# One PSUM bank of the mixer goes from the projections to the transposes of the attention weights

## The chip, the cores and the metric

The kernel runs on one core of a Trainium2 chip. The time is the device time of one launch, in microseconds (us), as the median of three runs. TensorE is PE in the profile, VectorE is DVE, ScalarE is ACT and GpSimd is POOL; PEld is the loading of PE's weights, which runs beside its matmuls. PE's results land in PSUM, which has eight banks; a bank holds 128 x 512 numbers of 32 bits, and ACT or DVE reads it out to SBUF.

## The reference

One layer of a hybrid block on 2048 tokens of width 1024, in float32:

```
h = rms_norm(x);  u = h @ w_in                    # 1024 -> 2560 columns: x, g, q, k, v
y_lru = gelu(u_g) * rg_lru(conv4(u_x))            # two 512 x 512 block-diagonal gates, a scan over tokens
z = q k^T / 8                                     # 8 heads of 64
att = exp(log_sigmoid(z) + suffix_sum(log_sigmoid(-z)))   # strictly causal, stick-breaking
y_att = att @ v
x = x + concat(rms_norm(y_lru), rms_norm(y_att)) @ w_out
x = x + swiglu(rms_norm(x)) @ w_ffn_out           # inner width 2816
out = rms_norm(x)
```

## The kernel before, in words

The first half of the kernel, up to about 1240 us, is the mixer: everything up to `w_out`. The rest is the FFN, which uses other PSUM pools.

Every matrix product is made of three matmuls with float32r operands, the high part times the high part and the two cross terms (`mm3`, lines 149 to 151). So each operand has to be split into a high part, which ACT copies, and a low part, which DVE or POOL subtracts.

The mixer works on four groups of 512 tokens. For each group, `prep` makes the projections. Its ten column groups stand in `GROUPS`: x, v, k, g, x, q, v, g, k, q. `make_ht` (line 207) turns the normalised tokens by PE transposes. `proj_col` (tile `pj`) makes one 128-column tile with 24 matmuls; `proj_v` (tile `pv`) makes one tile of values with 24 shorter ones; `Lru.gates` (tile `pg`) makes a gate tile with 3. Every one of these tiles, those of the transposes (`htp`, `h2t`), of the output projection (`po`) and of its sums (`pss`) is a bank of the pool `ps_d`. Such a bank is read out by ACT, DVE or both: a column of q or k by ACT line 290 and then DVE line 291; a tile of values by lines 315 and 316; a gate by ACT line 517; a turned tile by lines 208 and 209; an output tile by DVE line 671. The columns of x go by ACT line 495 into the convolution (ACT 498, DVE 500 three times, ACT 504).

The attention works on items: 128 queries by up to 512 keys. Each passes four stages, on different engines: `score` (matmuls into `z`, two sigmoids on ACT, a mask on POOL on the diagonal), `scan` (DVE line 372), `weights` (DVE line 378) and `turn`. `turn` (line 393) turns the weights by up to four PE transposes into a bank of the pool `ps_t` (tile `t`), which ACT copies (line 394, `ah`) and from which DVE subtracts (line 395, `al`). `weigh` then multiplies with the values into the one bank of `ps_y`. `LAGS` sets how far the stages run ahead: the scores four items before the turn.

`drive` interleaves the attention of group g with the projections of group g+1 (with the output projection for the last group), a few matmuls at a time. PE's order is exactly the order in which this is written. DVE, ACT, POOL and the DMA queue get their order from a scheduler, which takes the ready instruction of highest priority; attention steps get a priority ahead of their place. All engines then work strictly in that order. A pool does not hand out its banks in turn: a new tile gets a bank that is free, and its first matmul waits until the last reader of that bank's tile before is done.

Of the kernel before, what the change touches and what calls it, by code (L numbers as in the profile page):

```python
# [14 lines left out]
PSUM = bass.MemoryType.PSUM  # L15
# [75 lines left out]
def tile_block(ctx: ExitStack, tc: tile.TileContext, x, w_in, w_out, w_gu, w_dn,  # L91
# [62 lines left out]
    base = ExitStack()  # L154
# [1 line left out]
    htp = base.enter_context(tc.tile_pool(name="htp", bufs=KD, side="left"))  # L156
    wp = base.enter_context(tc.tile_pool(name="wp", bufs=WB, side="left"))
    stg = base.enter_context(tc.tile_pool(name="stg", bufs=4, side="left"))
    ps_d = base.enter_context(tc.tile_pool(name="ps_d", bufs=3, space=PSUM, side="left"))
    mix = ExitStack()  # L160
    lrp = mix.enter_context(tc.tile_pool(name="lrp", bufs=1, side="right"))
    atp = mix.enter_context(tc.tile_pool(name="atp", bufs=2, side="right"))
    kvp = mix.enter_context(tc.tile_pool(name="kvp", bufs=6, side="right"))
    ps_z = mix.enter_context(tc.tile_pool(name="ps_z", bufs=2, space=PSUM, side="right"))
    ps_t = mix.enter_context(tc.tile_pool(name="ps_t", bufs=2, space=PSUM, side="right"))
    ps_y = mix.enter_context(tc.tile_pool(name="ps_y", bufs=1, space=PSUM, side="right"))

    wg_hi = lrp.tile([P, NCT, 2, P], F32R, name="wg_hi")
# [1104 lines left out]
```

## Time and profile before

| | |
|---|---|
| runs | 2610.23, 2612.49, 2614.08 us; median 2612.49 us |
| profiled execution | 2616.12 us, span 2614.4 us |
| PE, PEld | 92%, 78% of the span busy |
| DVE, ACT, POOL | 70%, 48%, 45% |
| mean granted clock of PE | 0.97 of full |
| mixer | from 0 to about 1240 us |

The profiled execution is one launch. A row of the timeline says when an instruction (or a run of equal ones) started, how long it took, and in brackets how long its engine had been idle and what ended the wait. A row of the waits adds such idle times: total, how many, the longest. A busy share is an average over the span: what a change in one stage is worth has to be read in that stage.

### The profile page before, as it was taken

To read this page: it belongs to the slowest core of one execution; us is meant where nothing else is said; L and a number is where in the kernel's file an instruction comes from. 1 tells how busy PE (TensorE), PEld (TensorE's weight loads), DVE (VectorE), ACT (ScalarE), POOL (GpSimd) and SP (SyncE) were. 2 spreads that over 40 slices of the span, in tenths; PEclk is the share of its full clock that TensorE was granted. 3 is DMA by queue.
4 is the path that set the end of the run, shared out by engine and by line. 5 is a ranking of instruction groups with operands and counts; after the bars stand their busy time and mean duration, and the time that the engine had idled before them with its cause. 6 is when DMAs were issued, how large, how long until landed. Compare 5 with 4: busy or idle time off the path is not lost.

```text
span 2614.4 us, 36856 instructions
## 1 busy us (share of the span) xinstructions
PE 2417.2 (92%) x12680; PEld 2046.0 (78%) x12680; DVE 1837.1 (70%) x2569; ACT 1258.0 (48%) x2277; POOL 1174.2 (45%) x1397
## 2 busy tenths in 40 slices
PE   7999999998888887998799979979999999999998
PEld 5888788787778787888577758868888887788886
DVE  4566888999999999898645546686566562544557
ACT  5656677676766665665433323343333332332334
POOL 5855433223244221112565565464555454644443
PEclk9999999999999999999899989989999999999999
DMA  7787887664556565654333453252332326755563
GB/s 254 254 289 254 268 264 228 197 210 164 163 182 204 176 200 174 218 177 138 128 133 129 150 196 110 90 199 89 109 113 93 102 92 263 272 174 173 195 200 145
DMA packets 221804, 468.57 MB, mean 179 GB/s; under 512 B 22704, under 2 KB 63664, under 8 KB 221616
## 3 DMA queue, kind: packets, MB, share of 16 engines
q1 hardware_dynamic: 221616, 466.21, 53.1%
q8 instruction: 100, 1.64, 0.3%
q14 instruction: 88, 0.72, 0.1%
HBM read 333.74 MB, written 132.38 MB: 178 GB/s over the span
## 4 chain that ended last, share of the span: by engine, by line
PE 43%; DVE 3%; DMA 2%; POOL 2%; issue 2%; ACT 1%; SPq 0%; POOLq 0%; DVEq 0%; ACTq 0%
PE pw L151 5%; PE pw L150 5%; PE pw L149 5%; PE psc L149 3%; PE psa L149 3%; PE psc L150 3%; PE psc L151 3%; PE psa L150 3%; PE psa L151 3%; PE psd L149 3%; PE psd L150 3%; PE psd L151 3%; PE psb L149 1%; PE psb L150 1%; PE psb L151 1%
## 5 line engine op out<-in xcount | busy, mean ns | idle before, releaser
L360 POOL MEMSET u<- 128x1 f32 x320 | 31.2, 99 | 558.0 <-DVE u L372 393.4
L372 DVE TENSOR_TENSOR_SCAN u<-u,u,zero 128x513 f32<-128x513 f32 x192 | 255.5, 1332 | 9.0 <-ACT u L362 8.5
L393 PE MATMUL t<-ident,be 128*128 128x128 f32 x1088 | 180.2, 282 | 55.2 <-DVE al L395 46.2
L378 DVE TENSOR_TENSOR be<-be,u 128x512 f32<-128x512 f32 (+2 forms) x320 | 215.2, 675 | 17.0 <-POOL be L366 1.4
L362 ACT ACTIVATE u<-z 128x512 f32<-128x512 f32 (+2 forms) x320 | 172.4, 539 | 96.8 <-PE z L358 61.2
L149 PE MATMUL pj<-ht_hi,w_hi 128*128 128x512 f32 x512 | 214.9, 420 | 2.3 <-DVE sl L291 1.5
L394 ACT CAST ah<-t 128x512 fp32r<-128x512 f32 (+2 forms) x320 | 168.7, 527 | 87.0 <-PE t L393 81.6
L393 PEld LDWEIGHTS t<-ident,be 128*128 128x128 f32 x1088 | 131.7, 144 | 94.1 <-DVE al L395 60.5
L151 PE MATMUL pj<-ht_hi,w_lo 128*128 128x512 f32 x512 | 202.3, 395 | 0.0
L150 PE MATMUL pj<-ht_lo,w_hi 128*128 128x512 f32 x512 | 202.0, 395 | 0.0
L358 PE MATMUL z<-ks,qd 128*128 128x512 f32 (+2 forms) x640 | 191.1, 380 | 6.8 <-ACT be L363 5.2
L395 DVE TENSOR_TENSOR al<-t,ah 128x512 fp32r<-128x512 f32 (+2 forms) x320 | 191.1, 598 | 7.1 <-ACT ah L394 6.7
L1089 POOL TENSOR_TENSOR e<-c,c 128x512 f32<-128x512 f32 x110 | 158.7, 1451 | 50.5 <-DVE c L1080 36.8
L363 ACT ACTIVATE be<-z 128x512 f32<-128x512 f32 (+2 forms) x320 | 172.6, 539 | 0.2
L408 PE MATMUL y<-ah,vs 128*128 128x256 f32 x576 | 149.6, 290 | 13.9 <-DVE yp L418 13.9
L149 PE MATMUL po<-wo_hi,yhi 128*128 128x256 f32 x512 | 156.3, 305 | 0.0
L372 DVE TENSOR_TENSOR_SCAN u<-u,zero 128x129 f32<-128x129 f32 (+3 forms) x128 | 112.1, 877 | 57.0 <-POOL u L366 55.4
L1142 DVE TENSOR_TENSOR blo<-dr,bhi 128x1024 fp32r<-128x1024 f32 (+1 forms) x41 | 83.1, 2029 | 94.5 <-ACT bhi L1141 94.5
L1142 POOL TENSOR_TENSOR a0lo<-act,a0hi 128x1024 fp32r<-128x1024 f32 (+1 forms) x41 | 99.4, 2424 | 110.6 <-ACT a0hi L1141 110.6
L408 PE MATMUL y<-al,vs 128*128 128x256 f32 x576 | 147.2, 286 | 0.0
L150 PE MATMUL po<-wo_lo,yhi 128*128 128x256 f32 x512 | 146.6, 286 | 0.0
L151 PE MATMUL po<-wo_hi,ylo 128*128 128x256 f32 x512 | 146.6, 286 | 0.0
(283 smaller groups left out, 7564.3 us busy)
## 6 DMA issues: line engine op xcount, KB each, us to landing
r<-in_w_gu SPq DMA_DIRECT2D x88, 512.0 KB, 4.1
act<-act_d SPq DMA_DIRECT2D x68, 512.0 KB, 4.1
dr<-in_w_dn SPq DMA_DIRECT2D x59, 512.0 KB, 4.5
act_d<-e SPq DMA_DIRECT2D x110, 256.0 KB, 2.0
w_hi<-w_d SPq DMA_DIRECT2D x50, 512.0 KB, 4.7
w_lo<-w_d SPq DMA_DIRECT2D x50, 512.0 KB, 5.6
vs<-vs_d SPq DMA_DIRECT2D x80, 256.0 KB, 3.6
ks<-ks_d SPq DMA_DIRECT2D x80, 256.0 KB, 3.6
```

The costliest lines, as they stand in the source:

```text
L149: nc.tensor.matmul(ps, lhsT=w_hi, rhs=m_hi, start=first, stop=False, skip_group_check=more)
L150: nc.tensor.matmul(ps, lhsT=w_hi, rhs=m_lo, start=False, stop=False, skip_group_check=more)
L151: nc.tensor.matmul(ps, lhsT=w_lo, rhs=m_hi, start=False, stop=last, skip_group_check=more)
L358: nc.tensor.matmul(z[:, :nz], lhsT=qd[:, i, qs], rhs=kss[p.c][:, :nz], start=i == 0, stop=i == 1)
L362: nc.scalar.activation(u[:, :n], z[:, :n], AF.Sigmoid, scale=-SCALE)
L363: nc.scalar.activation(be[:, :n], z[:, :n], AF.Sigmoid, scale=SCALE)
L372: nc.vector.tensor_tensor_scan(out=ur, data0=ur, data1=zero.broadcast_to([P, n + 1]), initial=1.0 if p.prev is None else p.prev.u[s][:, 0: ...
L378: nc.vector.tensor_tensor(out=p.be[s][:, :n], in0=p.be[s][:, :n], in1=p.u[s][:, 1:n + 1], op=ALU.mult)
L393: nc.tensor.transpose(tp[:, b, :], p.be[s][:, b * P:(b + 1) * P], ident)
L395: nc.vector.tensor_tensor(out=alo[:, :nb, s, :], in0=tp[:, :nb, :], in1=f32(ahi[:, :nb, s, :]), op=ALU.subtract)
L408: nc.tensor.matmul(y, lhsT=vs[:, b, :], rhs=t[:, b].rearrange("p s q -> p (s q)"), start=first and m == 0, stop=last and m == 1)
L1142: eng.tensor_tensor(out=lo, in0=src, in1=f32(hi), op=ALU.subtract)
```

## The change

Of the eight banks of the mixer, `ps_d` had three, `ps_z` two, `ps_t` two and `ps_y` one. Now `ps_d` has two and `ps_t` three. Nothing is added or removed.

```
-    ps_d = base.enter_context(tc.tile_pool(name="ps_d", bufs=3, space=PSUM, side="left"))
+    ps_d = base.enter_context(tc.tile_pool(name="ps_d", bufs=2, space=PSUM, side="left"))
...
-    ps_t = mix.enter_context(tc.tile_pool(name="ps_t", bufs=2, space=PSUM, side="right"))
+    ps_t = mix.enter_context(tc.tile_pool(name="ps_t", bufs=3, space=PSUM, side="right"))
```

PE's instructions stand in the same order in both programs. The orders of DVE, ACT, POOL and the DMA queue differ in places. Two of ACT's and one of DVE's matter below.

On ACT at the start of the program, where the turned tokens of group 0 (`htp0_2` to `htp0_7`) are read out and the weights of the first projection are split:

```order
 L208 ACTIVATE ht_hi0_3_464<-htp0_3_466,gm_377 128x512
+L226 CAST w0_8_0_hi_534<-w0_8_0_raw_536 128x1024
 L208 ACTIVATE ht_hi0_4_473<-htp0_4_475,gm_377 128x512
-L226 CAST w0_8_0_hi_534<-w0_8_0_raw_536 128x1024
 L208 ACTIVATE ht_hi0_5_482<-htp0_5_484,gm_377 128x512
+L226 CAST w0_8_1_hi_543<-w0_8_1_raw_545 128x1024
 L208 ACTIVATE ht_hi0_6_491<-htp0_6_493,gm_377 128x512
 L208 ACTIVATE ht_hi0_7_500<-htp0_7_502,gm_377 128x512
-L226 CAST w0_8_1_hi_543<-w0_8_1_raw_545 128x1024
```

Two splits of weights have moved ahead of read-outs: the first by one read-out, the second by two.

On ACT at the end of the first group's projections, where the last column (`pj0_5_1`) and the last two turned tiles of group 1 are read out and the attention starts:

```order
 L290 CAST sh0_11_1705<-pj0_5_1_1626 128x512
 L208 ACTIVATE ht_hi1_6_1713<-htp1_6_1715,gm_377 128x512
+L208 ACTIVATE ht_hi1_7_1722<-htp1_7_1724,gm_377 128x512
 L362 ACTIVATE u0_0_0_0_0_1744<-z0_0_0_0_0_1741 128x128
 L363 ACTIVATE be0_0_0_0_0_1740<-z0_0_0_0_0_1741 128x128
-L208 ACTIVATE ht_hi1_7_1722<-htp1_7_1724,gm_377 128x512
```

The last tile's read-out has moved ahead of the first two sigmoids of the attention.

On DVE during the projections of group 1, where a column of k (`pj1_4_0`) is read out between the steps of the attention of group 0; the program before:

```order
L494 COPY xpad2_0_3975<-halo_252 128x3
L372 SCALAR_TENSOR_TENSOR u0_4_1_0_1_2785<-u0_4_1_0_1_2785,zero_67 128x513
L378 TENSOR_TENSOR be0_4_1_0_1_2781<-be0_4_1_0_1_2781,u0_4_1_0_1_2785 128x512
L418 TENSOR_TENSOR yp0_1_2544<-y0_3_0_0_2796,yb0_3_0_0_2801 64x256
L395 TENSOR_TENSOR al0_4_0_0_2820<-t0_4_0_0_0_2823,ah0_4_0_0_2819 128x128
L291 TENSOR_TENSOR sl1_8_2831<-pj1_4_0_2759,sh1_8_2830 128x512
L372 SCALAR_TENSOR_TENSOR u0_5_0_0_0_2856<-u0_5_0_0_0_2856,zero_67 128x129
```

The changed program has the same rows here, in the same order: the read-out `sl1_8` has not moved.

## Rows read from the trace of the kernel before

**Rows 1.** The page: busy time (share of the span) and instructions.
```profile
PE 2417.2 (92%) x12680; PEld 2046.0 (78%) x12680; DVE 1837.1 (70%) x2569; ACT 1258.0 (48%) x2277; POOL 1174.2 (45%) x1397
```

**Rows 2.** Windows: stretch, length, busy PE, PEld, DVE, ACT, POOL, PEclk, DMA share, GB/s.
```profile
27.00:150.00 123.00, 119.18 (x622) 100.97 (x621) 60.22 (x79) 68.84 (x103) 90.29 (x94) 1.00 0.79 263
150.00:300.00 150.00, 144.71 (x814) 123.58 (x814) 105.82 (x186) 96.71 (x202) 87.48 (x180) 1.00 0.79 266
300.00:520.00 220.00, 210.52 (x1263) 181.12 (x1261) 195.21 (x306) 151.01 (x313) 68.78 (x187) 0.99 0.74 238
520.00:800.00 280.00, 252.31 (x1499) 213.91 (x1497) 265.04 (x381) 195.79 (x385) 87.90 (x229) 0.98 0.56 182
800.00:1250.00 450.00, 385.97 (x2849) 361.20 (x2847) 412.54 (x677) 272.21 (x555) 105.18 (x261) 0.93 0.56 186
...
900.00:950.00 50.00, 38.60 (x267) 34.94 (x267) 43.41 (x84) 33.08 (x68) 6.70 (x28) 0.83 0.66 217
```

**Rows 3.** Waits of PE from 27 to 520 us: total us, times, longest.
```profile
PE t L393 <- DVE al L395: 5.6, 7, 1.2
```

**Rows 4.** Waits of PE from 520 to 1250 us.
```profile
PE t L393 <- DVE al L395: 40.6, 47, 2.8
...
PE h2t L713 <- DVE xo L707: 11.4, 2, 6.5
```

**Rows 5.** Waits of DVE from 520 to 1250 us.
```profile
DVE u L372 <- POOL u L366: 12.1, 14, 3.3
DVE u L372 <- ACT u L362: 5.7, 6, 1.4
DVE al L395 <- ACT ah L394: 5.3, 8, 1.0
```

**Rows 6.** Timeline of PE from 232 us: start, length, instruction, [idle before].
```profile
233.41 0.39 PE L149 MATMUL pj<-ht_hi,w_hi 128*128 128x512 f32 x1
...
239.64 0.39 PE L408 MATMUL y<-ah,vs 128*128 128x256 f32 x1 [0.56 <-DVE yp L418]
```

**Rows 7.** Timeline of ACT from 228 us.
```profile
236.20 0.62 ACT L504 CAST xh<-xc 128x512 fp32r<-128x512 f32 x1 [2.04 <-DVE xc L500]
...
237.40 0.59 ACT L290 CAST sh<-pj 128x512 fp32r<-128x512 f32 x1
```

**Rows 8.** Timeline of DVE from 228 us.
```profile
239.83 0.68 DVE L291 TENSOR_TENSOR sl<-pj,sh 128x512 f32<-128x512 f32 x1
```

**Rows 9.** Timeline of PE, then of DVE, at 20 us.
```profile
19.64 1.49 PE L207 MATMUL htp<-ident,xt 128*128 128x128 f32 x6
...
20.51 0.75 DVE L209 SCALAR_TENSOR_TENSOR ht_lo<-htp,gm,ht_hi 128x512 fp32r<-128x512 f32 x1 [0.34 <-ACT ht_hi L208]
```

**Rows 10.** Timeline of PE and DVE at 1238 us.
```profile
1238.57 0.28 PE L149 MATMUL po<-wo_hi,yhi 128*128 128x256 f32 x1
...
1239.25 0.74 DVE L671 SCALAR_TENSOR_TENSOR xo<-po,ry_y,xo 128x512 f32<-128x512 f32 x1
```

**Rows 11.** Timeline of PE from 90 us.
```profile
92.92 0.39 PE L149 MATMUL pj<-ht_hi,w_hi 128*128 128x512 f32 x1
...
99.13 0.28 PE L149 MATMUL pv<-w_hi,ht_hi 128*128 128x256 f32 x1
```

**Rows 12.** Timeline of DVE, then of ACT, from 88 us.
```profile
97.59 0.69 DVE L291 TENSOR_TENSOR sl<-pj,sh 128x512 f32<-128x512 f32 x1 [0.55 <-ACT sh L290]
...
103.03 0.69 ACT L517 ACTIVATE ig<-pg,lp 128x512 f32<-128x512 f32 x1
```

**Rows 13.** Timeline of PE, then of ACT and DVE, from 142.3 us.
```profile
143.95 0.66 PE L207 MATMUL htp<-ident,xt 128*128 128x128 f32 x4 [0.17 <-DVE sl L291]
...
145.14 0.60 PE L207 MATMUL htp<-ident,xt 128*128 128x128 f32 x4
...
144.64 0.69 ACT L208 ACTIVATE ht_hi<-htp,gm 128x512 fp32r<-128x512 f32 x1 [0.84 <-PE htp L207]
...
145.37 0.75 DVE L209 SCALAR_TENSOR_TENSOR ht_lo<-htp,gm,ht_hi 128x512 fp32r<-128x512 f32 x1 [0.78 <-ACT ht_hi L208]
```

## The prediction

> **What bounds the kernel now.** I read the page first, then the windows by stage, then the waits of PE and DVE, then the timeline around single PSUM tiles. PE is busy for 92% of the span, DVE for 70% [rows 1], but the stages differ. From 27 to 520 us PE is busy 119.2 of 123, 144.7 of 150 and 210.5 of 220 us, that is 96 to 97%, and DVE 49, 71 and 89%: PE is the bound, and a stall of PE there lengthens the kernel one for one. From 520 us DVE is at 265.0 of 280 and 412.5 of 450 us, PE at 90 and 86%: there DVE sets the pace, and the reader is to see that PE has room to wait [rows 2].
>
> The wait that the change takes aim at is PE's transposes waiting for `al`, the last reader of a `ps_t` bank. It is 5.6 us before 520 us [rows 3] and 40.6 us after it [rows 4]. So nearly nine tenths of it lie where PE isn't the bound. DVE's own waits there for work that comes from PE (`u`, by ACT or POOL, and `al`) are 12.1 + 5.7 + 5.3 = 23.1 us [rows 5]; more than that a freer PE cannot give back through DVE.
>
> **What the bank taken away costs.** In the changed program I took, for each tile of `ps_d`, the bank it is given and the tile that held it before. Of 246 such reuses 179 go to the tile two before, 41 to the one directly before (a column of 24 matmuls holds the other bank meanwhile); before, 182 went to the tile three before. I then read in the trace of before when that earlier tile's last reader ended and when the new tile's first matmul started. Where the reader ended later, PE will have to wait. I call the difference lateness.
>
> The largest: the second column of a k group starts at 233.41 [rows 6]. Its bank is now that of the first column, whose copy ACT makes at 237.40, behind an `xh` that waited 2.04 us for the convolution on DVE [rows 7]; DVE's subtraction runs from 239.83 for 0.68 us [rows 8]. It ends at 240.51, 7.1 us late. With three banks nobody waited for it. The scheduler could have moved that read-out forward, but its row stands where it stood: its order follows the priorities, not the banks.
>
> Counted so, 82 of 246 tiles are late, by 140.9 us in all. The first is the third turned tile at the start, in the row of six matmuls at 19.64, whose bank is free at 20.51 + 0.75 = 21.26 [rows 9]; the last is an output tile at 1238.57, whose bank is free at 1239.25 + 0.74 = 1239.99 [rows 10]. By stretch: 7 tiles and 6.1 us up to 27 us; 19 and 31.7 us up to 150; 12 and 32.1 us up to 300; 23 and 36.3 us up to 520; 21 and 34.7 us after that.
>
> Lateness isn't yet time, since a first wait moves what follows. Example: a column starts at 92.92, its bank is free at 97.59 + 0.69 = 98.28, 5.4 us late. A tile of values starts at 99.13 [rows 11], its bank is read until 103.03 + 0.69 = 103.72 [rows 12], 4.6 us late. If that read doesn't move, the first wait has covered the second and the pair costs 5.4; if it moves with PE, 10.0. It stands on ACT behind the read-out of the very column that was held up, so it moves in part; I put it at 1.7 us, which makes 6.3 of 10.0 us.
>
> The terms:
>
> - Start, 6.1 us late. All tiles wait for a bank, but the chain of DVE's 0.75 us read-outs limits it already. With two banks, two tiles take one round of 0.60 (PE) + 0.69 (ACT) + 0.75 (DVE) [rows 13] and 0.1 for handing over, 2.15 us, or 1.07 each against the 0.9 from start to start of now: 8 tiles, 1.4 us. ACT's two splits of weights, of 1024 columns where a read-out has 512 and takes 0.69 [rows 13], now stand ahead of read-outs; part of that hides in PE's and DVE's share of the round: I add 1.1. Together 2.5, between 1 and 6.
> - Turned tiles of groups 1 to 3 and the column after each, 25 tiles, 27.8 us late. The last column of q holds one bank, so each turned tile needs the bank of the one just before: 2.04 us and hand-offs instead of 1.19 from 143.95 to 145.14 [rows 13]. Such a wait follows work that PE has just done, so it moves with PE and nearly all of it is paid: 25, between 20 and 28. The read-out that ACT now makes before two sigmoids touches one of them.
> - The other 29 tiles between 27 and 520 us, 72.3 us late (columns, values, gates). Two thirds, as in the example: 48. It is also what comes out when of each of their 13 clusters in time only the largest is paid (7.1, 6.8, 5.4, 5.3 and so on down to 0.7: 47.6). Between 7 (one wait moves all of PE's work behind it, and no later read-out moves with it) and 72.
> - Off: 5.6 us of waits for `al` go [rows 3], and short waits like the 0.56 us for `yp` in the middle of the late column [rows 6] are covered by the longer ones: 3. Together 9.
> - After 520 us: 21 tiles, 34.7 us late, mostly output tiles that wait for DVE. They cost between 0 (DVE works on meanwhile; the scores run four items ahead) and 34.7; I take a third, 12, since DVE is the bound. The third `ps_t` bank gives between 0 and 23.1 us [rows 5]; I take half, 12. Net nothing, between -23 and +35.
> - Clock. Around the 6.5 us wait for `xo` [rows 4] the granted clock falls to 0.83 for 50 us [rows 2], which is 8.5 us of full-speed work. Six of the new waits are between 4.4 and 7.1 us long. I take 5, between 0 and 20.
>
> Sum: 2.5 + 25 + 48 - 9 + 0 + 5 = 71.5, say 72 us. The profiled execution took 2616.1 us, so its like would take 2688; the median of the runs lies 3.6 us lower, 2612.5, so the forecast is 2685. A difference under 0.2%, 5 us, cannot be told from none here.
>
> The FFN uses other pools and other banks of its own; it should move as a block.
>
> **A rule against this.** The repeated wait for `al` is 40.6 us in 47 pieces after 520 us [rows 4]. The Trainium skill, "Perfetto Trace Analysis", section "Optimization Strategy", says that the same gap coming back on the engine that should be saturated can mean that there isn't enough PSUM for the next tile. By that rule a third bank is the cure, and its result is the second rival below. The trace agrees that the bank is what PE waits for; it doesn't agree that PE is the engine to be saturated there.
>
> On the clock the skill's "TensorE: Matmul & The Clock Gate", section "HAM oscillation — how this bites in real kernels", says that gaps in PE's work throttle it, so that what follows starts slow. The trace agrees with 0.83 around the long wait [rows 2]; by the rule alone the clock's term would lie nearer to its upper end of 20.
>
> **The rivals.**
>
> - *Everything is paid.* Read-outs move with PE throughout, since ACT and DVE are fed by PE. Then 140.9 us less 9, and 10 for the clock, twice the forecast's: +142, 2754. For it: the read-outs sit behind attention steps that need PE. Against it: the example and DVE's pace after 520 us. 15%.
> - *The third bank pays more than the second cost.* After 520 us PE runs ahead, DVE's 23.1 us of waits go, and 5.6 us before; the late read-outs cost less than that because queues of ACT and DVE, shorter while PE stands, catch up. Then 2612.5 - 28.7 = 2584. It decides the sign only if the bank taken away costs under 28.7 us; the turned tiles alone come to at least 20, which is why it gets 5%.
> - *Stalls are absorbed.* Read-outs that wait for a DMA or stand in a queue of ACT or DVE keep their times while PE falls behind, so a late PE finds the next banks free: half of the 48 is paid, the other terms at their lower ends, 1 + 20 + 24 - 9 = +36, about 2650. Against it: ACT's queue is strict, and much of what stands in it waits for PE. 15%.
> - *The change does nothing.* It would need that the freed bank comes as early as before; the lateness shows the reverse. Within 5 us of 2612.5: 3%.
>
> **How the numbers follow.** The forecast gets 62%, with its own range 2655 to 2715: the terms at half of their distances. The wider range, 2640 to 2740, takes in most of the absorbed case and the lower part of the fully paid one, and leaves out about 2 in 10. Slower: 62 + 15 + 15 = 92%; the same 3%; faster 5%.
>
> **What would show it.** Right: PE's waits for `al` before its transposes fall from 46 us to under 10. New rows of PE waiting for `sl`, `vt`, `ig`, `ht_lo` and `xo` stand before `pj`, `pv`, `pg`, `htp` and `po`, some 60 to 100 us in all, with one of about 7 us at the k column near 233 us plus the shift so far. The attention of group 0 starts some 25 us later, the part up to the first tile of the last group some 65 us later, and the time from there to the FFN stays as long as it was. DVE's busy time doesn't change. Wrong: waits on `ps_d` under 40 us before 520; or the stretch after 520 us getting shorter by over 15 us, which would say that PE was the bound there after all; or many read-outs that ACT and DVE make earlier than their rows in the order let me expect.

## The result, and the profile after

The changed kernel takes 2684.78 us (median of 4 runs, 2682.09 to 2685.46), the kernel before beside it 2612.06: a ratio of 1.0274, interval 1.0257 to 1.029. Forecast were 2685 and a range of 2640 to 2740. The profiled execution took 2685.46 us, with a span of 2683.7.

The page's busy line, which answers to [rows 1]:

```profile
PE 2439.5 (91%) x12680; PEld 2065.9 (77%) x12680; DVE 1840.8 (69%) x2569; ACT 1260.3 (47%) x2276; POOL 1174.8 (44%) x1397
```

DVE, ACT and POOL are as busy as before. PE is busy 22.3 us longer with the same 12680 instructions. That is the first sign that waits are not the whole of the loss.

Windows of the changed kernel, with the columns of [rows 2]. The matmuls that ran at 520, 800 and 1250 us now run at 580, 860 and 1325:

```profile
29.00:580.00 551.00, 494.33 (x2698) 418.01 (x2699) 364.43 (x574) 318.60 (x615) 247.31 (x460) 0.97 0.70 227
580.00:860.00 280.00, 250.92 (x1501) 215.19 (x1501) 261.98 (x377) 194.93 (x384) 85.66 (x227) 0.97 0.56 178
860.00:1325.00 465.00, 393.22 (x2847) 370.67 (x2845) 416.00 (x678) 274.24 (x557) 106.44 (x263) 0.92 0.54 182
```

With the rows of before they make the account of the 69.3 us by which the span grew:

| stretch of before | length before, after | growth | forecast |
|---|---|---|---|
| start to 27 us | 27, 29 | +2 | +2.5 |
| 27 to 520 | 493, 551 | +58 | +64 (25 + 48 - 9), and most of the clock's 5 |
| 520 to 800 | 280, 280 | 0 | 0 for 520 to 1250 |
| 800 to 1250 | 450, 465 | +15 | (above) |
| 1250 to the end | 1364.4, 1358.7 | -6 | 0 |

The first cut doesn't quite match: the matmul that ran at 27.1 us now runs at 31.2, so about 2 of the 58 us belong to the start. The length and PE's busy time give the split of the +58. PE's idle time (length less busy) was 3.8 + 5.3 + 9.5 = 18.6 us [rows 2] and is 56.7: +38. Its busy time was 474.4 and is 494.3: +20.

PE's waits from 29 to 580 us (total us, times, longest), in place of [rows 3]:

```profile
PE pj L149 <- DVE sl L291: 15.9, 7, 5.2
PE htp L207 <- DVE ht_lo L209: 13.3, 14, 2.4
PE pj L149 <- ACT ig L517: 12.1, 4, 5.8
PE pg L149 <- DVE vt L316: 5.4, 5, 4.4
PE htp L207 <- DVE sl L291: 3.4, 3, 1.6
PE pv L149 <- ACT ig L517: 2.7, 2, 1.4
PE pv L149 <- ACT r L517: 1.4, 1, 1.4
PE pj L149 <- DVE ht_lo L209: 1.2, 2, 0.7
```

Every row is a tile of `ps_d` waiting for the last reader of another. They sum to 55.4 of the 56.7 us of idle time, so PE waits for little else any more, and no transpose of weights waits for `al`. Waits of this kind stood there before too, with three banks: these rows and three of 0.2 to 0.3 us, 6.0 us together.

```profile
PE pv L149 <- ACT ig L517: 2.0, 2, 1.6
PE htp L207 <- DVE ht_lo L209: 1.7, 3, 1.0
PE pj L149 <- DVE sl L291: 1.5, 2, 1.0
```

PE's waits from 580 to 1325 us, in place of [rows 4]:

```profile
PE po L149 <- DVE xo L671: 27.4, 13, 4.1
...
PE y L408 <- DVE yp L418: 15.0, 14, 2.4
PE t L393 <- DVE be L378: 8.1, 8, 2.0
```

And DVE's there, in place of [rows 5]:

```profile
DVE u L372 <- ACT u L362: 13.2, 16, 1.5
DVE u L372 <- POOL u L366: 13.2, 13, 3.3
DVE al L395 <- ACT ah L394: 9.0, 12, 3.0
```

The 40.6 us for `al` are gone, but PE waits as long for DVE at other places (`xo`, `yp`, `be`), and DVE's three waits are now 35.4 us where they were 23.1.

Three places that the forecast named. First the k column whose bank would come 7.1 us late; PE, with the columns of [rows 6]:

```profile
271.00 0.79 PE L149 MATMUL pj<-ht_hi,w_hi 128*128 128x512 f32 x1 [5.23 <-DVE sl L291]
271.59 0.63 PE L150 MATMUL pj<-ht_lo,w_hi 128*128 128x512 f32 x1
```

ACT and DVE before it, which answer to [rows 7, 8]:

```profile
266.67 0.62 ACT L504 CAST xh<-xc 128x512 fp32r<-128x512 f32 x1 [2.03 <-DVE xc L500]
...
267.87 0.59 ACT L290 CAST sh<-pj 128x512 fp32r<-128x512 f32 x1
```
```profile
266.75 1.22 DVE L372 TENSOR_TENSOR_SCAN u<-u,zero 128x513 f32<-128x513 f32 x1
...
270.26 0.68 DVE L291 TENSOR_TENSOR sl<-pj,sh 128x512 f32<-128x512 f32 x1
```

The chain is the one foreseen: `sh` stands behind `xh`, which waits for the convolution; `sl` stands behind four steps of the attention (`u`, `be`, `yp`, `al`). PE came to the column at 271.00 - 5.23 = 265.77, 32.4 us later than before; the bank came free at 270.94, 30.4 later than its 240.51. So nearly all of the read-out's time moved with PE, and 5.2 of the 7.1 us were waited.

Second, the pair of the example, a column and the tile of values after it [rows 11, 12]:

```profile
104.98 0.79 PE L149 MATMUL pj<-ht_hi,w_hi 128*128 128x512 f32 x1 [4.18 <-DVE sl L291]
...
110.21 0.39 PE L149 MATMUL pj<-ht_hi,w_hi 128*128 128x512 f32 x1
110.44 0.39 PE L150 MATMUL pj<-ht_lo,w_hi 128*128 128x512 f32 x1
...
115.11 0.39 PE L149 MATMUL pv<-w_hi,ht_hi 128*128 128x256 f32 x1 [1.27 <-ACT ig L517]
```

The waits are 4.18 + 1.27 = 5.45 us, where I had reckoned 6.3. But the twelve matmuls from 104.98 to 110.21 take 5.23 us, 0.44 each, where the same twelve take 0.23 each before the wait: 2.5 us more. The granted clock of 101 to 111 us is 0.66. PE came to the wait at 2.4 GHz and went on from it at 1.2 GHz.

Third, turned tiles of group 1, which answer to [rows 13]:

```profile
161.39 0.66 PE L207 MATMUL htp<-ident,xt 128*128 128x128 f32 x4 [1.62 <-DVE sl L291]
...
163.62 0.66 PE L207 MATMUL htp<-ident,xt 128*128 128x128 f32 x4 [0.87 <-DVE ht_lo L209]
```

One tile in 2.23 us: the round of 2.04 us and hand-offs, as forecast, where 1.19 stood before.

### The profile page after: what moved, and what is told of

Read it like the earlier page. It is cut to its first block, busy times and chain, and to the rows that moved or that the text cites. A ratio compares the mean times of both kernels' runs of the same rounds, so it can differ in the third digit from the quotient of the medians.

```text
span 2683.7 us, 36928 instructions
## 1 busy us (share of the span) xinstructions
PE 2439.5 (91%) x12680; PEld 2065.9 (77%) x12680; DVE 1840.8 (69%) x2569; ACT 1260.3 (47%) x2276; POOL 1174.8 (44%) x1397
## 4 chain that ended last, share of the span: by engine, by line
PE 42%; DVE 3%; DMA 2%; POOL 2%; issue 2%; ACT 1%; SPq 0%; POOLq 0%; DVEq 0%; ACTq 0%
PE pw L151 5%; PE pw L150 5%; PE pw L149 5%; PE psc L149 3%; PE psa L149 3%; PE psa L150 3%; PE psc L150 3%; PE psa L151 3%; PE psc L151 3%; PE psd L149 3%; PE psd L150 2%; PE psd L151 2%; PE psb L150 1%; PE psb L149 1%; PE psb L151 1%
## 5 line engine op out<-in xcount | busy, mean ns | idle before, releaser
L149 PE MATMUL pj<-ht_hi,w_hi 128*128 128x512 f32 x512 | 221.4, 432 | 37.5 <-DVE sl L291 21.3
L149 PE MATMUL po<-wo_hi,yhi 128*128 128x256 f32 x512 | 161.3, 315 | 28.2 <-DVE xo L671 27.4
```

Source lines behind the costliest of these rows:

```text
L149: nc.tensor.matmul(ps, lhsT=w_hi, rhs=m_hi, start=first, stop=False, skip_group_check=more)
```

## The experiments

The theory was: the loss is what PE waits for the two banks of `ps_d`, in the terms of the sum, and the third bank of `ps_t` gives some 12 us back. The rivals: the third bank gives nothing; the read-outs' place in the queues, not the number of banks, is what costs; the waits only move, since DVE is full. Differences to the changed kernel are between medians; the kernel before, run beside each, had medians from 2609.18 to 2612.55 us, so a difference of some 3 us between two runs says nothing.

**d2_t2: the bank taken away, and given to nobody.**

```
-    ps_t = mix.enter_context(tc.tile_pool(name="ps_t", bufs=3, space=PSUM, side="right"))
+    ps_t = mix.enter_context(tc.tile_pool(name="ps_t", bufs=2, space=PSUM, side="right"))
```

> Two banks for the projections as in the changed kernel, two for the transposes as before; one bank stays unused. It is the loss alone. Theory (the sum of the prediction): the third transposing bank gives back some 18 us (12 after 520 us, 5.6 before), so this is slower than the changed kernel by that, about 2703 us. Rival 1 (DVE sets the pace after 520 us and the columns' waits hide the rest): the third bank gives nothing, about 2685 us. Rival 2 (the wait for al is time): it gives all of 46 us, about 2730 us.

Measured: 2683.45 us, 1.028 of before (1.0263 to 1.0296), the same as the changed kernel, so the theory's 2703 is out. PE's waits from 580 to 1325 us, then DVE's:

```profile
PE t L393 <- DVE al L395: 36.1, 44, 2.3
PE po L149 <- DVE xo L671: 18.0, 9, 3.8
...
PE y L408 <- DVE yp L418: 3.9, 4, 1.7
...
PE t L393 <- DVE be L378: 2.2, 3, 0.9
```
```profile
DVE u L372 <- POOL u L366: 15.0, 15, 3.3
DVE u L372 <- ACT u L362: 12.2, 15, 1.4
DVE al L395 <- ACT ah L394: 7.3, 12, 1.8
```

The third bank takes 35.0 of the 36.1 us of waits for `al` away and gives 9.4 us to `xo`, 11.1 to `yp` and 5.9 to `be` (2.2 and 8.1): PE waits for the same engine a step later. PE's whole idle time from 580 to 1325 us is 99.9 us with two banks and 100.9 with three, and the last output tile starts at 1315.8 and 1314.0 us: in this stage the third bank is worth 2 us at most. DVE's own waits are 34.5 us with two banks of `ps_t` and 35.4 with three, so none of them was owed to that bank. Their rise from 23.1 [rows 5] comes with the bank that `ps_d` lost.

**turned_in_t: the changed kernel, with the turned tiles in `ps_t`.**

```
-            tp = ps_d.tile([P, GT], F32, tag="d", name=f"htp{g}_{k}")
+            tp = ps_t.tile([P, GT], F32, tag="t", name=f"htp{g}_{k}")
```

> The changed kernel, but the turned tokens of make_ht take their banks from ps_t (three) and no longer from ps_d (two). Theory: the chain of turned tiles that each wait for the one just before is a cost of its own; its waits (ht_lo 15.7 us against 2.3 before, sl 3.4, the column behind it 1.2) go, some 18 us, and a few us of half clock: about 2663 us. Rival: the wait only moves to the next column, or to the transposes of the attention that share the pool: 2680 to 2690 us.

Measured: 2658.7 us (1.0182, 1.0165 to 1.02), 26.1 less than the changed kernel; the terms for the start and the turned tiles were 2.5 + 25. The stretch that was 551 us long:

```profile
25.00:556.00 531.00, 488.50 (x2715) 416.96 (x2714) 369.50 (x578) 321.75 (x622) 250.61 (x465) 0.97 0.72 236
```

It begins 4 us earlier and is 20 us shorter, of which 14.2 are idle time (42.5 where 56.7 were) and 5.8 are busy time. The size was right, but not its make-up: waits make up less of it than forecast, and matmuls at the lower clock make up a part.

**readouts_early: the changed kernel, with all read-outs of `ps_d` 60 places of priority ahead.**

```
+            with tc.high_priority(offset=60):
                 nc.scalar.copy(hi.bitcast(F32R), ps)
                 nc.vector.tensor_tensor(out=lo, in0=ps, in1=hi, op=ALU.subtract)
```

(and so for lines 208 and 209, 315 and 316, 495, 517 and 671)

> The changed kernel, but every read-out of a ps_d bank gets a priority ahead of the attention's steps (60 places against 24), so that ACT and DVE make it earlier. Theory: the waits for sl, ig, vt and xo (21.3 + 14.9 + 5.7 + 27.4 us in the changed kernel) come from the place of the read-outs in strict queues; about half of them goes, 35 us, about 2650 us. Rival: the read-outs are late because what they need (a free SBUF tile behind a DMA, the convolution) is late, and an earlier place blocks the attention's instructions behind them: 2685 us or more.

Measured: 2676.3 us (1.025, 1.023 to 1.027), 8 less, where the theory had 35. PE's waits over the whole span:

```profile
PE y L411 <- DVE yp L421: 25.7, 18, 3.5
PE pj L149 <- DVE sl L293: 23.1, 10, 6.8
PE po L149 <- DVE xo L677: 22.0, 9, 4.1
```

The columns' waits for `ig` (14.9 us in the changed kernel) are gone, the columns' wait for `sl` is not (21.3 there), and `y` waits for `yp` 10 us longer. This order moves little; it doesn't show that no order could.

**xh_on_pool: the changed kernel, with the copy ahead of `sh` on another engine.**

```
-            nc.scalar.copy(xh, xc)
+            nc.gpsimd.tensor_copy(xh, xc)
```

> The changed kernel, but the rounded copy xh of the convolution is made by POOL instead of ACT. In the changed kernel ACT stood idle 2.0 to 3.8 us before an xh in the middle of its queue, with a read-out of a ps_d bank behind it (column at 105.0 us, which waited 4.2 us; column at 271.0 us, 5.2 us). Theory: part of the lateness is this strict queue, so without it the waits for sl and ig fall from 36 us to about 22, and the kernel takes about 2670 us. Rival 1: DVE's subtraction behind it is as late anyway (at 271.0 us it came 1.8 us after the copy): 2680 us or more. Rival 2: POOL takes 1.3 us and more for what ACT did in 0.62, the gates come later: slower than 2685 us.

Measured: 2683.19 us (1.0277, 1.0262 to 1.0292): no difference. POOL's copy took 0.61 us in the median, so it was not slower than ACT's 0.62. Over the whole span PE waits for `sl` as long as before, 20.8 us in 9 pieces. At the k column one sees why: `sh` no longer waits for the convolution and ends at 261.54 us, but `sl` still stands behind the same four steps of DVE, and PE waits 6.09 us for it.

```profile
260.95 0.59 ACT L290 CAST sh<-pj 128x512 fp32r<-128x512 f32 x1 [0.44 <-PE pj L151]
...
266.97 0.68 DVE L291 TENSOR_TENSOR sl<-pj,sh 128x512 f32<-128x512 f32 x1
```

**output_tiles_in_t: the changed kernel, with all output tiles but the last eight in `ps_t`.**

```
-                    po = ps_d.tile([P, GT], F32, tag="d", name=f"po{self.nm}_{n}_{t}")
+                    pool, tag = (ps_d, "d") if (self.g, self.br) == (NG - 1, 1) else (ps_t, "t")
+                    po = pool.tile([P, GT], F32, tag=tag, name=f"po{self.nm}_{n}_{t}")
```

> The changed kernel, but the output projection's tiles (po), all but the last 8, take their banks from ps_t (three) instead of ps_d (two). Before, the last group took 437 us from the first output tile to the last; in the changed kernel 454. Theory: those 16 us are PE's waits for xo (27.4 us), for want of a third bank while DVE's queue lies 3 to 7 us behind PE; with ps_t's banks most of them go, and the kernel takes about 2672 us, the stretch some 440 us. Rival: DVE is full there, so any three banks for both kinds of tile only move the wait to t or y: 2682 us or more.

Measured: 2678.14 us (1.0261, 1.0246 to 1.0276), 6.6 less. The 27.4 us for `xo` moved more than they went; PE's waits over the whole span:

```profile
PE t L393 <- DVE al L395: 15.9, 14, 2.1
PE po L149 <- DVE al L395: 12.3, 16, 2.9
...
PE t L393 <- DVE xo L672: 8.6, 9, 2.0
```

The stretch from the first output tile to the last was expected at 440 us and is 451 (437 before, 454 in the changed kernel), so the want of a third bank in `ps_d` is not by itself what makes it long.

**turned_and_output_in_t: both edits.**

The diffs are those of the two runs.

> Both the turned tiles of make_ht (alone 2658.7, 26 us less than the changed kernel) and the output tiles (alone 2678.1, 6.6 us less) take their banks from ps_t. Theory (the terms of the sum lie in different stages, so they add): 2684.8 - 26.1 - 6.6 = 2652. Rival (a wait of PE for DVE in the last group only moves, and part of the gain of the output tiles was chance): 2658, as with the turned tiles alone. What is left, 40 to 46 us above the program before, is then the columns, values and gates of ps_d and the clock.

Measured: 2656.91 us (1.0168, 1.0147 to 1.0189), 1.8 less than with the turned tiles alone. That is nearer to the rival's 2658 than to 2652, but the runs spread over 3 to 5 us: how much the output tiles give by themselves, between 2 and 7 us, stays open.

**one_pool_of_five: the five banks in one pool.** Against the program before:

```
-    ps_d = base.enter_context(tc.tile_pool(name="ps_d", bufs=3, space=PSUM, side="left"))
+    ps_d = base.enter_context(tc.tile_pool(name="ps_d", bufs=5, space=PSUM, side="left"))
...
-    ps_t = mix.enter_context(tc.tile_pool(name="ps_t", bufs=2, space=PSUM, side="right"))
...
-        tp = ps_t.tile([P, TPG, P], F32, tag="t", name=f"t{p.nm}_{s}")
+        tp = ps_d.tile([P, GT], F32, tag="d", name=f"t{p.nm}_{s}").rearrange("p (b q) -> p b q", q=P)
```

> Instead of three and two, or two and three: one pool of five banks from which projections and transposes both take. Theory: a bank goes where it is missing; neither the 46 us of waits for al nor those for late read-outs stand in full, but DVE still sets the pace after 520 us, so 5 to 20 us faster than the kernel before, about 2600 us. Rival: the transposes of the attention hold the banks in turn with slow columns, so a transpose waits for a column's read-out that lies behind attention steps: 2630 us or more.

Measured: 2599.41 us, 0.9957 of before (0.9941 to 0.9973): faster than both. The first two stretches, and PE's waits over the whole span:

```profile
25.00:514.00 489.00, 474.89 (x2702) 408.46 (x2701) 363.25 (x573) 317.99 (x619) 244.01 (x464) 0.99 0.77 255
514.00:793.00 279.00, 253.12 (x1504) 216.04 (x1503) 263.24 (x382) 195.83 (x386) 90.76 (x230) 0.97 0.57 181
```
```profile
PE y L407 <- DVE yp L417: 32.9, 20, 3.9
...
PE t L392 <- DVE be L377: 11.7, 11, 2.5
...
PE t L392 <- DVE sl L290: 3.0, 1, 3.0
```

Up to 514 us PE is idle for 14.1 us instead of 18.6; waits for the pool's banks are under 5 us of it, the longest the 3.0 of a transpose for `sl`. After that it waits for DVE's `yp` and `be` instead of `al`: the stretch is 279 where it was 280.

**one_pool_of_four: the same with four, one bank unused.**

> One bank fewer than before, changed kernel and one_pool_of_five, all tiles of ps_d and ps_t in one pool of four. Theory (what costs is that a bank is tied to a kind of tile, not how many there are): before 520 us few transposes of weights are in flight, so three of the four are mostly free for the columns, as before the change; some 10 to 35 us slower than one_pool_of_five (2599.4): 2610 to 2635, so faster than the changed kernel by over 45 us although it has one bank less. Rival (the number of banks decides): four shared banks are worse than five split ones: about 2685 or more, with waits on PE for sl and ht_lo as in the changed kernel.

Measured: 2620.21 us (1.0039, 1.0026 to 1.0052), 64.6 us less than the changed kernel, which has one bank more. Its first stretch, and the largest of its waits for the pool's banks, over the whole span (the profiled execution was the longest of ten, 2628.93 us):

```profile
25.00:529.00 504.00, 478.54 (x2696) 410.62 (x2694) 364.65 (x573) 318.92 (x619) 247.92 (x464) 0.98 0.75 247
```
```profile
PE t L392 <- DVE al L394: 30.2, 34, 2.3
...
PE pj L149 <- DVE al L394: 11.3, 7, 5.1
```

It has as many banks for these tiles as d2_t2, which splits them two and two and takes 2683.45 us. So what costs here is less that a bank is missing than that banks are tied to one kind of tile.

**one_pool_of_seven** (also the scores' two banks in the pool) and **one_pool_xh_on_pool** (five banks and the copy of `xh` on POOL):

> One pool of seven banks for projections, transposes and scores (z had two of its own). Theory: with five shared banks PE's waits for a projection's or a transpose's bank are down to a few us (3.0 + 2.7 in the profile) and those for a score's bank at 10 us; only these can go, and DVE sets the pace there: within 5 us of 2599. Rival: scores that run ahead take banks from the projections or the transposes: 2610 us or more.

> The pool of five banks (2599 us), and xh made by POOL as well. If ACT's queue is what makes read-outs late, the pool has already covered it: no difference, 2595 to 2602 us. If read-outs still hold PE up, some us faster, 2590. If POOL's slower copy delays the gates, slower: 2605 us or more.

Measured: 2601.63 us (0.9965, 0.9951 to 0.9979) and 2605.43 us (0.9976, 0.9965 to 0.9987). Neither is better than five banks in one pool, which stays the fastest version.

## Why the prediction was right, point by point

The sum was 71.5 us and the span grew by 69.3, so the direction, the size and most of the place are right. By the medians it is 72.7: the profiled execution of before was 4.1 us above the median of its runs, the one after 0.7 us. But several of the terms were wrong, and that their errors cancel to within 2 us is luck. The range 2655 to 2715 was said to be the terms at half of their distances; added, these halves give 2647 to 2725.

- *Start, 2.5 (1 to 6).* The first column starts at 29.31 us instead of 26.10: 3.2. Right; but its first matmuls run at half pace, which costs 2.7 us more by 35.3 us and is in none of the start's terms.
- *Turned tiles, 25 (20 to 28).* Their waits and those of the column behind them are 13.3 + 3.4 + 1.2 = 17.9 us, of which 1.9 stood there before: 16, under the range. What taking them out of `ps_d` gives is 26.1 us, start included. The price was right and the term counted the wrong thing: beside the waits there is a price in clock.
- *The other 29 tiles, 48 (7 to 72).* The five other rows of waits sum to 37.5 us, of which 4.1 stood there before: 33 of 72.3 us of lateness, under half of it and not two thirds. At the k column the read-out moved with PE for 30.4 of 32.4 us, so it is not that read-outs kept their times. The share of the lateness that is paid was the step that failed here, by 15 us; the clock and the last group are off by as much the other way.
- *Off, 9.* Of PE's 18.6 us of idle time before, 6.0 were waits for banks of `ps_d` already. Of the other 12.6, 1.3 are left (56.7 - 55.4): 11.3 are gone, so the term was nearly right. I had counted the waits for `al` and two or three that I had seen; with PE late at most tiles, nearly everything else that it used to wait for is early.
- *After 520 us, 0 (-23 to +35).* It was +15, all of it in the last group. The gain was put at 12 of 23.1 us; d2_t2 shows 2 at most. The loss was put at 12; it is about 15. From the first output tile to the last it takes 454 us in the changed kernel, 453 in d2_t2 and 451 with the output tiles in `ps_t`, but 440 and 439 with one pool of five or four and 437 before. DVE's waits rose by 12.3 us; that this is because PE, held up at an output tile, comes late to the scores that DVE needs is argued from the order of PE, not shown by a run of its own. That DVE sets the pace there was right, and I drew only half of the conclusion: a bank that PE waits for, where DVE is the bound, moves the wait and gives nothing.
- *Clock, 5 (0 to 20).* PE's busy time grew by 20 us between 27 and 520 us alone, and at 104.98 us it can be seen how: 2.5 us after a wait of 4.18. I had scaled one long wait of before [rows 2, 4]. Between 29 and 580 us the clock fell to 1.2 GHz eight times, where it did so once between 27 and 520 us of before, and it stayed there 33 us longer in all. Five of the eight came at single waits of 3.4 to 5.8 us, three at turned tiles with waits of 0.3 to 2.4 us. Those 33 us at half pace cost at most 16.5 us, and the slow start adds 2.7: up to 19 of the 20. So the term lies at its upper end. That is where the rule of the Trainium skill, "TensorE: Matmul & The Clock Gate", section "HAM oscillation — how this bites in real kernels", would have put it; here the trace agrees in that the clock fell at gaps, by a granted clock of 0.97 over a stretch that had 0.99 and 1.00.
- *FFN.* It was to move as a block and is 6 us shorter. From the last matmul of the output projection to the end the kernels shown take 1362 to 1375 us with the same instructions (before 1373, changed 1367). What makes the difference was not settled, so of the gain of one_pool_of_five (9.8 us against the 2609.18 of before beside it) only the 7.5 by which its last output tile starts earlier (1231.0 instead of 1238.6 us) are explained by the banks. The mixer by itself grew by 75 us in the changed kernel.

Net of each other: new waits 49.4 instead of 73, less 11.3 instead of 9, which is 38 instead of 64; clock 20 instead of 5; after 520 us +15 instead of 0; FFN -6 instead of 0.

The rivals. *Everything is paid* (2754) is out: half was paid. *Stalls are absorbed* (2650) had the waits more nearly right (its terms for 27 to 520 us give 20 + 24 - 9 = 35, measured 38), but for another reason than it named, and without the clock and the last group its time was too low. *The third bank pays more* is refuted by d2_t2. The Trainium skill, "Perfetto Trace Analysis", section "Optimization Strategy", reads a repeated gap on the engine that should be saturated as a possible want of PSUM. Here the bank was indeed what PE waited for, but PE was not the engine to be saturated (90 and 86% busy against DVE's 95 and 92 [rows 2]), and giving the bank changed the time by 2 us at most.

Of the signs promised: waits for `al` under 10 us (1.1), the new waits of 60 to 100 us (55.4 before 580 us; with the 27.4 for `xo` and the 5.5 for `sl` after it, 88), attention of group 0 about 25 us later (+26), DVE's busy time unchanged. The last group was to start 65 us later (59) and keep its length (it didn't).

## What to carry to other kernels

Before a buffer is moved between pools, compute for each tile of the pool that loses it when its new bank comes free; take about half of that lateness as waits where the engine is the bound (here 49 of 100 us), and add what the clock loses behind the waits. Then ask of the gain whether the engine that waits is the bound in that stage: if it is not, the wait goes one step on. And before splitting banks another way, try one pool for all tiles of a size: here four shared banks came within 0.4% of the better split of five, and five shared ones beat it by as much.

## What the runs showed of the hardware

A wait of 4.18 us in the middle of matmuls at 2.4 GHz was followed by twelve matmuls at half the pace (0.44 us instead of 0.23 from start to start), at a granted clock of 0.66 over the ten microseconds around it; so a single stall of this length cost 2.5 us, more than half of itself, once it was over. The 5.23 us before the k column did the same to the matmuls behind it (0.63 us each where 0.40 is usual), at 0.83 from 268 to 278 us.

At the start of the program a window's granted clock can mislead. The first column in the timeline of PE, changed kernel, and a window over it:

```profile
29.31 0.80 PE L149 MATMUL pj<-ht_hi,w_hi 128*128 128x512 f32 x1 [0.71 <-DVE ht_lo L209]
29.90 0.63 PE L150 MATMUL pj<-ht_lo,w_hi 128*128 128x512 f32 x1
```
```profile
29.00:34.00 5.00, 4.69 (x11) 3.74 (x12) 1.00 (x2) 1.37 (x2) 3.06 (x4) 1.00 0.78 236
```

Matmuls of 0.63 us follow one another up to 35 us, the pace of 1.2 GHz, while the granted clock of 29 to 34 us is given as 1.00. The trace has no record of the clock before 35.04 us, and what has no record counts as full. In the kernel before the record begins at 22.50 us, at full clock, in the middle of twelve transposes that follow one another without a wait; the changed kernel waits 0.7 to 1.0 us before every eight. With the turned tiles in `ps_t` (turned_in_t) it begins at 22.28 us again. So where the record begins, and the busy time of equal instructions, told more here than the mean of a window.
